# A fused encoder step: probabilities by key block with the sinks as a score column, and the sums' reciprocals as a power on GpSimd

## The chip, the cores and the metric

One core of one Trainium2 chip runs the whole step. The metric is the device time of one execution in microseconds (us). Engines are called as in the profile: PE is TensorE, DVE is VectorE, ACT is ScalarE, POOL is GpSimd, SP is SyncE (it only issues DMAs). "L434" is line 434 of the kernel; the changed kernel has its own line numbers.

## The reference

One layer, 320 rows (256 of a new stream and 64 of a running one), width 2048, in fp32. A combined projection `z = rmsnorm(x) @ W_in` gives queries, keys, values and the gMLP's two halves. The attention has 16 heads of 64 channels, two key/value heads, chunks of 64 rows that see their own and the two chunks before, a relative-position bias and a learned sink per head:

```python
def sink_attention(q, k, v, bias, sinks, valid=None):
    s = jnp.einsum('...qhgd,...khd->...hgqk', q, k).astype(jnp.float32) * (HEAD_DIM ** -0.5) + bias
    if valid is not None:
        s = jnp.where(valid, s, NEG_INF)
    sink = sinks.astype(jnp.float32)[..., None]
    m = jnp.maximum(jnp.max(s, axis=-1), sink)
    p = jnp.exp(s - m[..., None])
    w = p / (jnp.sum(p, axis=-1, keepdims=True) + jnp.exp(sink - m)[..., None])
    return jnp.einsum('...hgqk,...khd->...qhgd', w.astype(v.dtype), v)
```

Queries and keys are RMS-normalised per head. The gMLP half normalises `v`, mixes it over 128 positions and gates `u` with it. Both results are normalised, joined and projected by `W_out` with a residual, then comes a squared-ReLU MLP of width 8192 with its residual.

## The kernel before

Everything is kept transposed: channels on the 128 partitions, the 320 rows along the free dimension. To reach fp32 precision, every weight piece of 4 x 128 x 256 is split into a high part (`w_hi`, by ACT, L115) and a rest (`w_lo`, by DVE, L116), the activations likewise, and each weight block takes three matmuls of 128x128 by 320 columns (L141; L237 for the first). `product` makes 256 output columns from 16 such blocks in four pieces; there are 8160 of these wide matmuls, and they run in one stream from the start to the end.

All smaller PE work is put between pieces of that stream by hand: `between_pieces` names functions that run behind the given piece, and `issue_after` fixes the order. What stands on DVE, ACT and POOL is ordered by a scheduler at build time from a model of the durations; on the chip each engine works through its list strictly in that order.

Attention works on ten units: five query chunks (64 keys, 128, and three times 192) for each of two key/value heads. `attend(i)` is called twice per 256 projected columns and does three things on PE: it transposes the probabilities of unit i-2 into two `misc` banks (L472), forms the scores of unit i in two banks (L420), and multiplies the transposed probabilities of unit i-3 with the values (L485). There are only two `misc` banks and two score banks, so each attend needs those of the one before to be emptied. Behind the PE part of unit i comes `softmax`, on the other engines: DVE scales the scores by the queries' norms and adds the bias into a tile `s` (L434, two buffers), takes the maximum over the keys (L438), joins it with the sinks, negates it and forms the sinks' distance (L440 to L444); ACT takes the exponentials with their sums `den` (L449) and that of the sink (L445); DVE adds the two and takes the reciprocal (L451, L452); POOL multiplies all of `s` by it in one instruction (L453). At the end ACT and DVE add up the values' two halves into `ao` (L495, L497), and DVE copies the transposed probabilities out of the `misc` banks (L501).

Between the attends lie the v columns of the gMLP: `gelu2` (DVE L518, L521 and L524, ACT, POOL L522), the sums of squares `acc_v` (POOL L513) and the gains (POOL L541). Behind the last attend, `rows_norm` makes the row norms of v (DVE L169, a power on POOL L171), and `by_rows` transposes v in two groups (L553), which ACT evicts with those norms as scale (L555).

Another power runs on POOL for the queries' norms (L334), 20 values per partition.

Of the kernel before, what the change touches and what calls it, by code (L numbers as in the profile page):

```python
# [15 lines left out]
P = 128  # L16
# [14 lines left out]
def hymba_step_kernel(ctx: ExitStack, tc: tile.TileContext, i, o):  # L31
# [53 lines left out]
    nc.gpsimd.dma_start(out=tab, in_=i["table"].rearrange("b h -> h b"))  # L85
    inv_1k = const.tile([P, 1], F32, name="inv_1k")
# [16 lines left out]
    loads, between, rests, steps, narrow, carry = [], [], [], [], [], []  # L103
# [18 lines left out]
    def products(w, k0, nk, c0, ps, rh, rl, deep=None, between_pieces={}, halves_behind={}):  # L122
# [6 lines left out]
        for a in range(0, nk, 4):  # L129
# [3 lines left out]
            with tc.issue_after(halves_behind[a // 4]()) if a // 4 in halves_behind else nullcontext():  # L133
                high, low = halves(raw, hi, lo)
# [39 lines left out]
    def two_parts(acc):  # L174
        hl = sm.tile([P, 2, T], F32R, name="n_hl", tag="w2", bufs=4)
        hi, lo = hl[:, 0], hl[:, 1]
        nc.scalar.activation(out=hi, in_=acc, func=AF.Copy)
        rests.append(nc.vector.tensor_tensor(out=lo, in0=acc, in1=hi.bitcast(F32), op=ALU.subtract).ins)
        return hi, lo

# [112 lines left out]

    kv = sm.tile([P, 2, T], F32, name="kv", tag="w2", bufs=4)
    with tc.issue_after(steps[-1][0]):
# [5 lines left out]
    def evict_q(g, q_ps):  # L301
# [11 lines left out]
        nc.scalar.activation(out=sq, in_=qg, func=AF.Square)  # L313
        return sq

    q_dram = dram.tile([2, 2, 2, 2, T], F32, name="q_dram")
    r_at = lambda g, b, p: (g // 2) * 20 + p * 10 + (g % 2) * 5 + b

    def norm_q(h, sqs):

        st = misc()
        for c in range(4):
            mm = nc.tensor.matmul(out=st[c * 32:(c + 1) * 32, 0:T], lhsT=hone, rhs=sqs[c // 2][:, :, c % 2], start=True, stop=True)  # L323
        narrow.append(mm.ins)
        rows = sm.tile([P, T], F32, name="q_rows", tag="w1", bufs=3)
        nc.scalar.activation(out=rows, in_=st[:, 0:T], func=AF.Copy)
# [11 lines left out]
    v0, v64, v128, vC, vD, w2, w3, w4 = (vz[:, x] for x in range(8))  # L338

# [24 lines left out]
    nc.scalar.activation(out=ksq, in_=zk, func=AF.Square)  # L364
    q0_sq = evict_q(0, q0_ps)
# [3 lines left out]
    def first_norms():  # L369
        rstd(ksq, mean_hd, EPS, rk)  # L370
        q1_sq.append(evict_q(1, q1_ps))

    def keys():
        for dst, c in ((kn[:, 0:256], slice(0, 256)), (kn[:, 384:448], slice(256, 320))):
            nc.vector.scalar_tensor_tensor(out=dst, in0=zk[:, c], scalar=g_k, in1=rk[:, c], op0=ALU.mult, op1=ALU.mult)
        for h in range(2):
# [8 lines left out]
        values(0, 1)  # L385

    q2_ps = product(w_in, 0, KT, 512, xh, xl,
                    between_pieces={0: first_norms, 1: lambda: norm_q(0, (q0_sq, q1_sq[0])), 2: keys, 3: lambda: values(2, 3, 4, 5)},
                    halves_behind={1: lambda: q0_out})
# [5 lines left out]
        (0, 0, 64, 128, None, (v0, w2)),  # L395
# [354 lines left out]
```

## Time and profile before

| | |
|---|---|
| median of 3 runs | 1239.93 us (1239.65 to 1240.73) |
| the profiled execution | 1239.04 us, span 1237.3 us |
| PE busy | 1232.8 us, 100% of the span |
| DVE, ACT, POOL busy | 663.6, 492.0, 114.0 us |
| chain that ended last | 99% PE, 93% of it `acc` L141 |
| clock of PE granted | full speed over the whole span |

The span is that of the traced instructions; the time also holds 1.7 us around it. In the groups, "idle before" is the time in which an engine had nothing to do ahead of these instructions, and what it waited for. In timelines the columns are start, duration, engine, line, operation, output and inputs with shapes; the bracket tells a wait and what ended it. Durations include the time in which an instruction stands still after it has started.

### The profile page before, as it was taken

How to read it: one execution, taken by the hardware profiler on the slowest of the kernel's cores; microseconds unless marked ns; L12 is line 12 of the kernel's file. 1: busy time of each engine (PE TensorE's matmuls, PEld its weight loads, DVE VectorE, ACT ScalarE, POOL GpSimd, SP SyncE). 2: the span in 40 equal slices, each digit the busy share in tenths (PEclk: the TensorE clock that was granted, in tenths of full speed). 3: DMA queues.
4: the chain of work that ended last, by engine and by line, in shares of the span. 5: the costliest groups of instructions: out<-in, count | busy, mean ns of one | idle time of the engine just before them, and what ended most of it. 6: DMA issues, size and time to landing. Idle time of an engine off the chain costs nothing.

```text
span 1237.3 us, 20626 instructions
## 1 busy us (share of the span) xinstructions
PE 1232.8 (100%) x8666; PEld 1225.0 (99%) x8666; DVE 663.6 (54%) x796; ACT 492.0 (40%) x652; POOL 114.0 (9%) x139
## 2 busy tenths in 40 slices
PE   9999999999999999999999999999999999999998
PEld 9999999999999999999999999999999999999998
DVE  7877778877864444444444444444444434444343
ACT  7446566435534432333434332344432333433321
POOL 3127454102200000000000000000000000000000
PEclk9999999999999999999999999999999999999999
DMA  9753346444555444454444444455444454445540
GB/s 282 226 148 104 104 138 195 153 154 141 151 152 153 153 147 145 152 154 149 146 149 153 154 150 143 151 154 152 147 147 151 154 151 144 150 152 164 172 161 33
DMA packets 187934, 188.03 MB, mean 152 GB/s; under 512 B 7616, under 2 KB 187376, under 8 KB 187840
## 3 DMA queue, kind: packets, MB, share of 16 engines
q1 hardware_dynamic: 186544, 185.48, 48.7%
q0 software_dynamic: 864, 0.98, 0.4%
q8 instruction: 68, 1.11, 0.4%
q10 hardware_dynamic: 432, 0.24, 0.1%
q14 instruction: 26, 0.21, 0.1%
HBM read 183.10 MB, written 3.35 MB: 151 GB/s over the span
## 4 chain that ended last, share of the span: by engine, by line
PE 99%; DVE 0%; issue 0%; ACT 0%; DVEq 0%
PE acc L141 93%; PE q_ps L237 1%; PE misc L141 1%; PE acc L237 1%; PE s_ps L420 1%; PE misc L472 0%; PE misc L83 0%; PE misc L485 0%; PE s_ps L485 0%; PE g_ps L566 0%; PE misc L566 0%; PE misc L553 0%; PE misc L323 0%; ACT s L449 0%; ACT w_hi L115 0%
## 5 line engine op out<-in xcount | busy, mean ns | idle before, releaser
L116 DVE TENSOR_TENSOR w_lo<-w_raw,w_hi 128x1024 fp32r<-128x1024 f32 x332 | 416.0, 1253 | 422.7 <-ACT w_hi L115 414.1
L115 ACT ACTIVATE w_hi<-w_raw 128x1024 fp32r<-128x1024 f32 x332 | 351.8, 1060 | 670.9 <-PE acc L141 646.7
L141 PE MATMUL acc<-H2H,w_lo 128*128 128x320 f32 x1024 | 316.4, 309 | 0.0
L141 PE MATMUL acc<-H2H,w_hi 128*128 128x320 f32 x1024 | 316.4, 309 | 0.0
L141 PE MATMUL acc<-H2L,w_hi 128*128 128x320 f32 x1024 | 316.4, 309 | 0.0
L141 PE MATMUL acc<-FH,w_hi 128*128 128x320 f32 x992 | 306.5, 309 | 0.0
L141 PE MATMUL acc<-FL,w_hi 128*128 128x320 f32 x992 | 306.5, 309 | 0.0
L141 PE MATMUL acc<-FH,w_lo 128*128 128x320 f32 x992 | 306.5, 309 | 0.0
L141 PEld LDWEIGHTS acc<-H2H,w_hi 128*128 128x128 f32 x1024 | 192.2, 188 | 0.0
L141 PEld LDWEIGHTS acc<-H2L,w_hi 128*128 128x128 f32 x1024 | 192.2, 188 | 0.0
L141 PEld LDWEIGHTS acc<-H2H,w_lo 128*128 128x128 f32 x1024 | 192.2, 188 | 0.0
L141 PEld LDWEIGHTS acc<-FH,w_hi 128*128 128x128 f32 x992 | 186.2, 188 | 0.0
L141 PEld LDWEIGHTS acc<-FL,w_hi 128*128 128x128 f32 x992 | 186.2, 188 | 0.0
L141 PEld LDWEIGHTS acc<-FH,w_lo 128*128 128x128 f32 x992 | 186.2, 188 | 0.0
L141 PE MATMUL acc<-XH,w_hi 128*128 128x320 f32 x352 | 110.7, 314 | 0.0
L141 PE MATMUL acc<-XH,w_lo 128*128 128x320 f32 x352 | 108.8, 309 | 0.0
L141 PE MATMUL acc<-XL,w_hi 128*128 128x320 f32 x352 | 108.7, 309 | 0.0
L141 PEld LDWEIGHTS acc<-XH,w_hi 128*128 128x128 f32 x352 | 66.1, 188 | 3.1 <-issue 3.0
L141 PEld LDWEIGHTS acc<-XL,w_hi 128*128 128x128 f32 x352 | 66.1, 188 | 0.0
L141 PEld LDWEIGHTS acc<-XH,w_lo 128*128 128x128 f32 x352 | 66.1, 188 | 0.0
L658 DVE SCALAR_TENSOR_TENSOR tf<-acc,r 128x640 f32<-128x640 f32 x32 | 26.4, 824 | 41.8 <-PE acc L141 41.8
L673 DVE TENSOR_TENSOR xT<-xT,acc 128x640 f32<-128x640 f32 x31 | 25.5, 821 | 41.8 <-PE acc L141 41.8
(227 smaller groups left out, 1086.3 us busy)
## 6 DMA issues: line engine op xcount, KB each, us to landing
w_raw<-in_w_up SPq DMA_DIRECT2D x128, 512.0 KB
w_raw<-in_w_down SPq DMA_DIRECT2D x128, 512.0 KB
w_raw<-in_w_in SPq DMA_DIRECT2D x44, 512.0 KB
w_raw<-in_w_out SPq DMA_DIRECT2D x32, 512.0 KB
w_first<-in_w_in SPq DMA_DIRECT2D x14, 256.0 KB
out_yT<-xT SPq DMA_DIRECT2D x7, 320.0 KB
xT<-in_xT SPq DMA_DIRECT2D x8, 160.0 KB
xT<-in_xT SPq DMA_DIRECT2D x4, 320.0 KB
```

Source lines behind the costliest of these rows:

```text
L115: return (pin(nc.scalar.activation(out=hi, in_=raw, func=AF.Copy)).ins, pin(nc.vector.tensor_tensor(out=lo, in0=raw, in1=hi.bitcast(F32), ...
L116: pin(nc.vector.tensor_tensor(out=lo, in0=raw, in1=hi.bitcast(F32), op=ALU.subtract)).ins)
L141: mm = nc.tensor.matmul(out=out, lhsT=w_[:, k, g * P:(g + 1) * P], rhs=r_(kk), start=(kk == 0 and x == 0), stop=(kk == nk - 1 and x == 2))
L237: mm = nc.tensor.matmul(out=ps[:, 0:T], lhsT=w_[:, j, k, g * P:(g + 1) * P], rhs=r_(a + k), start=(a + k == 0 and x == 0), stop=(a + k == ...
L420: mm = nc.tensor.matmul(out=s_ps[p][x * HD:(x + 1) * HD, j * nk:(j + 1) * nk], lhsT=qT[hs, blk_, a + x], rhs=kz[hs, kv, k0:k0 + nk], start ...
L658: nc.vector.scalar_tensor_tensor(out=t, in0=ps[:, :, 0:T], scalar=0.0, in1=r2[:, None, :].to_broadcast([P, 2, T]), op0=ALU.max, op1=ALU.mult)
L673: nc.vector.tensor_tensor(out=xT[:, a, c], in0=xT[:, a, c], in1=p, op=ALU.add)
```

## The change

The scores' tile `s` gets one more key column that holds the sinks, copied by DVE (L444 of the changed kernel). The maximum is taken over keys and sink at once, already negated, and the exponentials with their sums run over the sink's column too. So the steps for the sink alone, the addition and DVE's reciprocal go. The reciprocal is a power of -1 on POOL (L457), from a constant tile `minus`. POOL then writes the probabilities into a new tile `pr` in two instructions (L461), ordered by blocks of 64 keys. `s` has one buffer in place of two, `pr` has two.

The transposes take one block of 64 keys for each half of the partitions (L483: 64 rows by 128 columns of weights, 64 columns of output), so that each value half is multiplied and summed in its own bank, and `ao` needs one copy per half in place of copy and addition. The value tiles are made from three transposes in place of six, moved out by four ACT copies. The parts of two sums of squares are formed earlier, and the second `norm_q` runs in the same place as `attend(2)`.

The diff, cut to what is spoken of:

```diff
@@ -83,6 +83,8 @@
         nc.tensor.matmul(out=warm_ps[:, 0:256], lhsT=nc.const_aps.tensor(0.0, [P, P], F32),
                          rhs=nc.const_aps.tensor(0.0, [P, 256], F32), start=True, stop=True)
     nc.gpsimd.dma_start(out=tab, in_=i["table"].rearrange("b h -> h b"))
+    minus = const.tile([P, 2, 2], F32, name="minus")
+    nc.vector.memset(minus, -1.0)
...
-    kzv = blk("kzv", [P, 2304])
+    kzv = blk("kzv", [P, 2560])
...
-    vz = kzv[:, 896:1920].rearrange("p (x h d) -> p x h d", x=8, h=2)
-    cv = i["cv"].rearrange("k (h d) -> k h d", h=2)
-    between.extend(((vz[:, 3], cv), (vz[0:HD, 4], cv[HD:P]), (vz[HD:P, 7], cv[0:HD])))
+    vz = kzv[:, 896:1792].rearrange("p (x h d) -> p x h d", x=7, h=2)
+    cv = i["cv"].rearrange("(x k) (h d) -> k x h d", x=2, h=2)
+    between.extend(((vz[0:HD, 5:7], cv), (vz[HD:P, 5:7], cv)))
...
-        with tc.issue_after(steps[min(8 + k // 2, 11)][0]):
+        with tc.issue_after(steps[min(5 + k // 2, 11)][0]):
             nc.scalar.activation(out=sq, in_=xT[:, k:k + 2], func=AF.Square)
...
-    def values(*xs):
-        for x, vps in zip(xs, [score_bank(1, "vps"), misc()] if len(xs) == 2 else banks(4)):
-            t0 = (0, 64, 128, -64, 192, 256)[x]
-            n = min(P, T - t0)
-            with tc.issue_after(narrow[-1]):
-                mm = nc.tensor.transpose(out=vps[0:n, 0:P], in_=kvx[:, 448 + t0:448 + t0 + n], identity=ident)
-            narrow.append(mm.ins)
-            for dst, r in (((v0, slice(0, P)), (w3, slice(HD, P))), ((v64, slice(0, P)),),
-                           ((v128, slice(0, P)), (w2, slice(0, HD))), ((w2, slice(HD, P)),),
-                           ((w3, slice(0, HD)), (vD, slice(HD, P))), ((w4, slice(0, HD)),))[x]:
-                nc.vector.tensor_copy(out=dst[r], in_=vps[r, 0:P].rearrange("k (h d) -> k h d", h=2))
-
-
-    q1_ps = product(w_in, 0, KT, 256, xh, xl, between_pieces={0: lambda: rstd(ssq, mean_dm, EPS, rx)},
-                    halves_behind={2: lambda: rests[-1]})
+    def values():
+        with tc.issue_after(narrow[-1]):
+            vps = score_bank(1, "vps").rearrange("k (x d) -> k x d", x=4)
+            for x, (t0, n) in enumerate(TT):
+                mm = nc.tensor.transpose(out=vps[0:n, x], in_=vT[:, t0:t0 + n], identity=ident)
+        narrow.append(mm.ins)
+        turned[:] = [vps]
+
+    def values_out():
+        vps = turned[0]
+        low, high = slice(0, HD), slice(HD, P)
+        for dst, to, of in ((low, 0, low), (high, 1, high), (high, 0, low), (low, 1, high)):
+            with tc.issue_after(turned[1]):
+                nc.scalar.activation(out=vz[dst, to:5:2].rearrange("k x h d -> k x (h d)"), in_=vps[of, 0:3 - to], func=AF.Copy)
+
...
     q2_ps = product(w_in, 0, KT, 512, xh, xl,
-                    between_pieces={0: first_norms, 1: lambda: norm_q(0, (q0_sq, q1_sq[0])), 2: keys, 3: lambda: values(2, 3, 4, 5)},
-                    halves_behind={1: lambda: q0_out})
+                    between_pieces={0: first_norms, 1: lambda: (values(), norm_q(0, (q0_sq, q1_sq[0])), values_out()), 2: keys},
+                    halves_behind={1: lambda: (q0_out, *parts_k[2:4])})
...
@@ -425,80 +439,72 @@
         blk_, kv = units[u]
         q0, k0, nk, b0 = blocks[blk_][0:4]
         js = slice(2 * kv, 2 * kv + 2)
-        s = at.tile([P, 2, 2, 192], F32, name="s", tag="s", bufs=2)
-
-        sv = s[:, :, :, 0:nk] if nk > HD else \
-            s.rearrange("x p j k -> x p (j k)")[:, :, P:2 * P].rearrange("x p (j k) -> x p j k", j=2)
+        s = at.tile([P, 2, 2, 193], F32, name="s", tag="s", bufs=1)
+        sv, se = s[:, :, :, 0:nk], s[:, :, :, 0:nk + 1]
+        nc.vector.tensor_copy(out=s[:, :, :, nk], in_=sinks_pj[:, :, js])
         for p in range(2):
             for j in range(2):
                 nc.vector.scalar_tensor_tensor(out=sv[:, p, j], in0=s_ps[p][:, j * nk:(j + 1) * nk],
                                                scalar=rq[:, r_at(2 * kv + j, blk_, p):r_at(2 * kv + j, blk_, p) + 1],
                                                in1=bias[:, p, 2 * kv + j, b0:b0 + nk], op0=ALU.mult, op1=ALU.add)
-        m = at.tile([P, 2, 2], F32, name="m", tag="m")
-        nc.vector.tensor_reduce(out=m, in_=sv, axis=AX.X, op=ALU.max)
-        sk = sinks_pj[:, :, js]
-        nc.vector.tensor_tensor(out=m, in0=m, in1=sk, op=ALU.max)
         nm = at.tile([P, 2, 2], F32, name="nm", tag="nm")
-        nc.vector.tensor_scalar(out=nm, in0=m, scalar1=-1.0, scalar2=None, op0=ALU.mult)
-        es = at.tile([P, 2, 2], F32, name="es", tag="es")
-        nc.vector.tensor_tensor(out=es, in0=sk, in1=m, op=ALU.subtract)
-        nc.scalar.activation(out=es, in_=es, func=AF.Exp)
+        nc.vector.tensor_reduce(out=nm, in_=se, axis=AX.X, op=ALU.max, negate=True)
         den = at.tile([P, 2, 2], F32, name="den", tag="den")
         for p in range(2):
             for j in range(2):
-                nc.scalar.activation(out=sv[:, p, j], in_=sv[:, p, j], func=AF.Exp, bias=nm[:, p, j:j + 1],
+                nc.scalar.activation(out=se[:, p, j], in_=se[:, p, j], func=AF.Exp, bias=nm[:, p, j:j + 1],
                                      accum_out=den[:, p, j:j + 1])
-        nc.vector.tensor_tensor(out=den, in0=den, in1=es, op=ALU.add)
-        nc.vector.reciprocal(out=den, in_=den)
-        ready[:] = [nc.gpsimd.tensor_tensor(out=sv, in0=sv, in1=den[:, :, :, None].to_broadcast([P, 2, 2, nk]),
-                                            op=ALU.mult).ins]
-        probs[u] = s
+        nc.gpsimd.tensor_tensor(out=den, in0=den, in1=minus, op=ALU.pow)
+        pr = at.tile([P, 2, 3, 2, HD], F32, name="pr", tag="pr", bufs=2)
+        ns = nk // HD
+        for p in range(2):
+            ready[:] = [nc.gpsimd.tensor_tensor(out=pr[:, p, 0:ns].rearrange("x n j k -> x j n k"),
+                                                in0=sv[:, p].rearrange("x j (n k) -> x j n k", k=HD),
+                                                in1=den[:, p, :, None, None].to_broadcast([P, 2, ns, HD]), op=ALU.mult).ins]
+        probs[u] = pr
 
     def attend(i):
 
         t, v = i - 2, i - 3
         t, v = t if 0 <= t < 10 else None, v if 0 <= v < 10 else None
-        bank = [misc(), misc()] if t is not None else None
-        s_ps = [score_bank(p) for p in range(2)]
+        bank = [misc(), misc()] if t is not None else [score_bank(r) for r in range(2)]
+        s_ps = [score_bank(p) for p in range(2)] if i < 10 else None
+        hs = [slice(r * HD, (r + 1) * HD) for r in range(2)]
 
         def behind(mms):
             with tc.issue_after(narrow[-1]):
                 narrow.append([mm() for mm in mms][-1].ins)
 
         if t is not None:
-            s = probs.pop(t).rearrange("x p j k -> x p (j k)")
-            nk = blocks[units[t][0]][2]
-            cols = ((P, 2),) if nk == HD else ((0, 0), (192, 1)) if nk == P else ((0, 0), (256, 1), (P, 2))
-            behind([lambda p=p, x=x, c=c: nc.tensor.transpose(out=bank[p][:, x * P:(x + 1) * P], in_=s[:, p, c:c + P],
-                                                              identity=ident) for p in range(2) for c, x in cols])
+            s = probs.pop(t)
+            subs = range(len(blocks[units[t][0]][4]))
+
+            def turn(p, n, x):
+                return nc.tensor.transpose(out=bank[x][:, (p * 3 + n) * HD:(p * 3 + n + 1) * HD],
+                                           in_=s[hs[x], p, n].rearrange("x j k -> x (j k)"), identity=ident[hs[x], hs[x]])
+
+            behind([lambda p=p, n=n, x=x: turn(p, n, x) for p in range(2) for n in subs for x in range(2)])
         if i < 10:
             behind([lambda: scores(i, s_ps)])
         if v is not None:
             blk_, kv = units[v]
-            q0, va, vb = (blocks[blk_][x] for x in (0, 4, 5))
-            hs = [slice(r * HD, (r + 1) * HD) for r in range(2)]
-            side = {(r, j): bank[r][:, 384:512] if bank and j == 0 else s_ps[r][:, 384:512] if j else s_ps[r][:, 0:P]
-                    for r in range(2) for j in range(2)}
-
-            def part(r, j, p, span):
-                lhsT, c = (va[j][hs[r], kv], slice(j * P, (j + 1) * P)) if span < 2 else (vb[j][hs[j], kv], slice(256, 384))
-                return nc.tensor.matmul(out=side[r, j][hs[p]], lhsT=lhsT, rhs=pts[v % 2][p][hs[r], c],
-                                        start=span < 2 or va is None, stop=span == 2 or vb is None or r != j)
-
-            turns = [x for x in (0, 2, 1) if (va, va, vb)[x] is not None]
-            behind([lambda r=r, p=p, x=x: part(r, 1 - r if x == 1 else r, p, x) for x in turns for r in range(2) for p in range(2)])
+            q0, tiles = blocks[blk_][0], blocks[blk_][4]
+            side = [b[:, 384:512] for b in bank]
+            behind([lambda n=n, x=x, j=j, p=p: nc.tensor.matmul(out=side[j][hs[p]], lhsT=vz[hs[j], x, kv],
+                                                                rhs=pts[v % 2][hs[j], :, p, n], start=n == 0,
+                                                                stop=n == len(tiles) - 1)
+                    for n, x in enumerate(tiles) for j in range(2) for p in range(2)])
         if i < 10:
             softmax(i, s_ps)
         if v is not None:
             for j in range(2):
                 dst = ao[:, 4 * kv + 2 * j:4 * kv + 2 * j + 2, q0:q0 + 64]
-                nc.scalar.activation(out=dst, in_=side[j, j].rearrange("p (a q) -> p a q", a=2), func=AF.Copy)
-                if va is not None:
-                    nc.vector.tensor_tensor(out=dst, in0=dst, in1=side[1 - j, j].rearrange("p (a q) -> p a q", a=2), op=ALU.add)
+                nc.scalar.activation(out=dst, in_=side[j].rearrange("p (a q) -> p a q", a=2), func=AF.Copy)
         if t is not None:
-            for p in range(2):
-                c = slice(min(x for _, x in cols) * P, (max(x for _, x in cols) + 1) * P)
-                nc.vector.tensor_copy(out=pts[t % 2][p][:, c], in_=bank[p][:, c])
+            for x in range(2):
+                ns = slice(0, len(subs))
+                nc.vector.tensor_copy(out=pts[t % 2][:, x, :, ns],
+                                      in_=bank[x][:, 0:384].rearrange("k (p n q) -> k p n q", p=2, n=3)[:, :, ns])
 
     q3_ps = product(w_in, 0, KT, 768, xh, xl,
                     between_pieces={1: lambda: attend(0), 3: lambda: attend(1)})
@@ -528,11 +534,10 @@
         return at.tile([P, TP], F32, name=name, tag="ssq_rows", bufs=1)
 
     acc_v = sums_rows("acc_v")
-    gvs = at.tile([P, 8, HD], F32, name="gvs", bufs=1)
+    gvs = room[:, 2048:2560].rearrange("p (a t) -> p a t", a=8)
     for g in range(4):
         v_ps = product(w_in, 0, KT, 2304 + g * 256, xh, xl, between_pieces={
-            1: lambda: attend(2 * g + 2), 2: lambda: norm_q(1, (q2_sq, q3_sq)) if g == 0 else None,
-            3: lambda: attend(2 * g + 3)})
+            1: lambda: (attend(2 * g + 2), norm_q(1, (q2_sq, q3_sq)) if g == 0 else None), 3: lambda: attend(2 * g + 3)})
         gelu2(v_ps, gv[:, 2 * g:2 * g + 2])
         for a in range(2 * g, 2 * g + 2):
             add_square(acc_v, gv[:, a], a == 0)
```

On POOL, around the product of unit 5 (64 keys; `gv` and `acc_v` are gains and sums of the v columns, `den` the sums of the exponentials), there stood:

```order
L522 TENSOR_TENSOR gc<-gc,z 128x640
L541 TENSOR_SCALAR gvs<-gv,cols 128x64 x2
L513 TENSOR_TENSOR acc_v<-acc_v,sq 128x320
L541 TENSOR_SCALAR gv<-gv,cols 128x256 x2
L513 TENSOR_TENSOR acc_v<-acc_v,sq 128x320
L453 TENSOR_TENSOR s<-s,den 128x2x128
L453 TENSOR_TENSOR s<-s,den 128x4x128
```

and now:

```order
L528 TENSOR_TENSOR gc<-gc,z 128x640
L546 TENSOR_SCALAR vnat<-gv,cols 128x64 x2
L457 TENSOR_TENSOR den<-den,minus 128x4
L519 TENSOR_TENSOR acc_v<-acc_v,sq 128x320
L546 TENSOR_SCALAR gv<-gv,cols 128x256 x2
L461 TENSOR_TENSOR pr<-s,den 128x128 x2
L519 TENSOR_TENSOR acc_v<-acc_v,sq 128x320
L457 TENSOR_TENSOR den<-den,minus 128x4
L461 TENSOR_TENSOR pr<-s,den 128x2x2x64 x2
```

The gains and one sum, which ran ahead of the product and needed nothing of the unit, now stand between the unit's power and its two products.

On DVE, at the next unit (128 keys, `attend(6)`), there stood:

```order
L116 TENSOR_TENSOR w_lo<-w_raw,w_hi 128x1024
L434 SCALAR_TENSOR_TENSOR s<-s_ps_1606,rq,bias 128x128 x2
L501 COPY kzv<-misc 128x384
L434 SCALAR_TENSOR_TENSOR s<-s_ps_1605,rq,bias 128x128 x2
L497 TENSOR_TENSOR ao<-ao,misc 128x2x64
L501 COPY vnat<-misc 128x384
```

and now:

```order
L118 TENSOR_TENSOR w_lo<-w_raw,w_hi 128x1024 x2
L444 COPY s<-sinks 128x4
L447 SCALAR_TENSOR_TENSOR s<-s_ps_1586,rq,bias 128x128 x2
L447 SCALAR_TENSOR_TENSOR s<-s_ps_1587,rq,bias 128x128 x2
L506 COPY kzv<-misc 128x384
L451 TENSOR_REDUCE nm<-s 128x4
L506 COPY kzv<-misc 128x384
```

The copy of the sinks into the single `s` stands ahead of the score evictions and of both bank copies. In the units of 192 keys a part of the weights has its place inside that stretch (unit 8):

```order
L444 COPY s<-sinks 128x4
L118 TENSOR_TENSOR w_lo<-w_raw,w_hi 128x1024
L447 SCALAR_TENSOR_TENSOR s<-s_ps_1831,rq,bias 128x192 x2
L447 SCALAR_TENSOR_TENSOR s<-s_ps_1832,rq,bias 128x192 x2
L506 COPY kzv<-misc 128x2x128 x2
```

where before `w_lo` stood ahead of the evictions and nothing tied these to POOL's product of the unit before. On POOL, behind the last unit's softmax, two `acc_v` sums and a copy (L513, L542) that stood ahead of its product now follow it (L519, L547), ahead of the `gc` of the first u columns.

More of the change, by code (lines that the diff above doesn't have):

```diff
@@ L100, in hymba_step_kernel @@
     nc.vector.memset(hone[HD:P, 1:2], 1.0)
-    loads, between, rests, steps, narrow, carry = [], [], [], [], [], []
+    firsts, loads, between, rests, steps, narrow, carry = [], [], [], [], [], [], []
     def load(out, in_):
@@ L132, in products @@
             load(raw, wv[:, k0 + a:k0 + a + 4, c0:c0 + 256])
-            with tc.issue_after(halves_behind[a // 4]()) if a // 4 in halves_behind else nullcontext():
+            with ExitStack() as order:
+                for ins in halves_behind[a // 4]() if a // 4 in halves_behind else ():
+                    order.enter_context(tc.issue_after(ins))
                 high, low = halves(raw, hi, lo)
@@ L176, in two_parts, with parts_of @@
         hi, lo = hl[:, 0], hl[:, 1]
-        nc.scalar.activation(out=hi, in_=acc, func=AF.Copy)
+        firsts.append(nc.scalar.activation(out=hi, in_=acc, func=AF.Copy).ins)
         rests.append(nc.vector.tensor_tensor(out=lo, in0=acc, in1=hi.bitcast(F32), op=ALU.subtract).ins)
         return hi, lo
+    def parts_of(acc):
+        hi, lo = two_parts(acc)
+        return hi, lo, firsts[-1], rests[-1]
     def rstd(acc, mean, eps, out):
@@ L321, in norm_q @@
         st = misc()
-        for c in range(4):
-            mm = nc.tensor.matmul(out=st[c * 32:(c + 1) * 32, 0:T], lhsT=hone, rhs=sqs[c // 2][:, :, c % 2], start=True, stop=True)
+        with tc.issue_after(narrow[-1]):
+            for c in range(4):
+                mm = nc.tensor.matmul(out=st[c * 32:(c + 1) * 32, 0:T], lhsT=hone, rhs=sqs[c // 2][:, :, c % 2], start=True,
+                                      stop=True)
         narrow.append(mm.ins)
         rows = sm.tile([P, T], F32, name="q_rows", tag="w1", bufs=3)
-        nc.scalar.activation(out=rows, in_=st[:, 0:T], func=AF.Copy)
+        turned.append(nc.scalar.activation(out=rows, in_=st[:, 0:T], func=AF.Copy).ins)
         for c in range(4):
@@ L405, in hymba_step_kernel @@
     probs, ready = {}, []
-    room = blk("vnat", [P, 2432])
+    room = blk("vnat", [P, 2560])
     vnat = room[:, 0:2048].rearrange("p (t c) -> p t c", t=2)
-    pt1 = at.tile([P, 768], F32, name="pt1", bufs=1)
-    pts = [(kzv[:, 1920:2304], room[:, 2048:2432]), (pt1[:, 0:384], pt1[:, 384:768])]
+    pts = [kzv[:, 1792:2560].rearrange("k (x p n q) -> k x p n q", x=2, p=2, n=3),
+           at.tile([P, 2, 2, 3, HD], F32, name="pt1", bufs=1)]
     def scores(u, s_ps):
```

25 lines of the change are left out of this document (15 added, 10 removed).

## The prediction

> **What bounds the kernel now.** I read the page first: its busy times and its chain.
>
> ```profile
> span 1237.3 us, 20626 instructions
> PE 1232.8 (100%) x8666; PEld 1225.0 (99%) x8666; DVE 663.6 (54%) x796; ACT 492.0 (40%) x652; POOL 114.0 (9%) x139
> PE 99%; DVE 0%; issue 0%; ACT 0%; DVEq 0%
> ```
>
> TensorE (PE) is the whole chain. Then the windows: one far behind the attention, and one over the stretch in which eight of the ten attention units run.
>
> ```profile
> 400.00:800.00 400.00, 400.00 (x2730) 400.00 (x2729) 173.61 (x156) 139.15 (x140) 0.00 (x0) 1.00 0.48 150
> 90.00:180.00 90.00, 89.66 (x846) 85.17 (x845) 72.71 (x149) 51.90 (x138) 54.61 (x48) 1.00 0.41 116
> ```
>
> A weight matmul costs 400/2730 = 146.5 ns; the change leaves all of these in place. So it can act in two ways only: the few PE instructions that attention puts into this stream change price, or another engine becomes so late that PE stands still. In 90 to 180 us DVE is busy 81% and POOL 61%, so the second way is near. The timeline of PE at one `attend` (first wide row to last) shows the first way:
>
> ```profile
> 130.99 0.31 PE L141 MATMUL acc<-XH,w_lo 128*128 128x320 f32 x1
> 131.14 0.38 PE L472 MATMUL misc<-ident,s 128*128 128x128 f32 x2
> 131.45 0.88 PE L420 MATMUL s_ps<-kzv,qT 64*64 64x192 f32 x16
> 132.92 0.41 PE L141 MATMUL acc<-XH,w_hi 128*128 128x320 f32 x1
> 133.17 0.31 PE L141 MATMUL acc<-XL,w_hi 128*128 128x320 f32 x1
> 122.00 0.82 PE L472 MATMUL misc<-ident,s 128*128 128x128 f32 x6
> 148.77 0.82 PE L472 MATMUL misc<-ident,s 128*128 128x128 f32 x6
> L472 PE MATMUL misc<-ident,s 128*128 128x128 f32 x48 | 7.1, 273 | 0.3 <-DVE vnat L501 0.3
> ```
>
> Two things to see. Six transposes take 0.82 us, one 0.273: a spacing of (0.82 - 0.273)/5 = 0.11 us. And the only wait of PE here, 0.3 us, is for a DVE copy (L501) that empties a `misc` bank. Three attends lie between 122.00 and 148.77: PE needs one every 8.92 us, and that is the time the other engines have for a softmax.
>
> **The change, part by part.** *PE's own work.* 48 transposes become 48 pairs, on the two row halves. No row shows such a pair. The nearest: score matmuls on four quarters, 16 records in 0.88 us, run together. If a pair does too, streaming 64 columns instead of 128, it takes about 0.065 us and 48 x 0.045 = 2.1 us go; at most half, 2.6; nothing if weight loading keeps 0.11 per pair. The new tile shape adds a change of shape at each of ten attends. Leaving the quarters costs 133.17 - 132.92 - 0.147 = 0.10 us behind the first wide matmul and some 0.05 to 0.1 ahead of it, so 0.15 x 10 = +1.5 (0 to +1.8). The values' six transposes become three (-0.33), and the second `norm_q` shares the attend's group (-0.15). Sum -1.1, between -3.1 and +1.3 (+6.6 if halves do not overlap at all: 48 x 0.11 more).
>
> *Instructions taken off DVE and ACT.* Per unit five four-element DVE operations, two additions to `ao` and an exponential go; a four-element copy comes. Nothing of these is on PE's chain, so by themselves they are worth 0.
>
> *POOL and the single buffer.* Before, `s` had two buffers. Now it has one: the copy of the sinks of unit u+1 must wait for POOL's writing of `pr` of unit u. Behind that copy on DVE stand the unit's score evictions, the bank copies (now L506) and later `w_lo` parts; the next attend's transposes wait for those banks. On POOL a power now stands ahead of `pr`, and in places gains and sums between the two. Their prices:
>
> ```profile
> L453 POOL TENSOR_TENSOR s<-s,den 128x768 f32<-128x768 f32 x6 | 8.8, 1468 | 5.3 <-PE misc L485 3.3 <-DVE den L452 1.9
> L453 POOL TENSOR_TENSOR s<-s,den 128x256 f32<-128x256 f32 x2 | 2.2, 1105 | 4.9 <-DVE den L452 4.9
> L334 POOL TENSOR_TENSOR rq<-r_q,nhalf 128x20 f32<-128x20 f32 x2 | 7.6, 3820 | 2.0 <-DVE r_q L333 1.9
> 105.56 4.07 POOL L334 TENSOR_TENSOR rq<-r_q,nhalf 128x20 f32<-128x20 f32 x1
> 178.47 1.79 POOL L171 TENSOR_TENSOR rs_rows<-r_rows,nhalf 128x3 f32<-128x3 f32 x1 [0.50 <-DVE r_rows L169]
> 178.31 1.21 DVE L116 TENSOR_TENSOR w_lo<-w_raw,w_hi 128x1024 fp32r<-128x1024 f32 x1
> 179.45 0.28 DVE L497 TENSOR_TENSOR ao<-ao,s_ps 128x128 f32<-128x128 f32 x1
> ```
>
> No row has a power of four elements. The shorter one of 20 took 2 x 3.82 - 4.07 = 3.57 us. The one of three took 1.79, but a `w_lo` ran beside it until 179.45; if it stood behind that, its own part is 178.47 + 1.79 - 179.45 = 0.81. Through 0.81 at three and 3.57 at 20 four give 0.97 us, which I take (bounds 0.8 and 1.9). The products: 1.47 us for 768; of the two for 256 one took 1.60 (next fence), so the other 0.61. That is 0.19 + 0.00166 per element, and half-size pieces cost 0.40 and 0.83. The added POOL work per unit is 0.97 + 0.19 = 1.16 us.
>
> *The first late unit.* Unit 5 (64 keys), timelines of DVE, ACT and POOL:
>
> ```profile
> 123.36 0.19 ACT L449 ACTIVATION_READ_ACCUMULATOR s<-s,nm 128x1 f32 x1
> 121.22 0.88 POOL L513 TENSOR_TENSOR acc_v<-acc_v,sq 128x320 f32<-128x320 f32 x1
> 122.08 2.37 POOL L541 TENSOR_SCALAR gv<-gv,cols 128x256 f32<-128x256 f32 x2
> 125.26 1.60 POOL L453 TENSOR_TENSOR s<-s,den 128x256 f32<-128x256 f32 x1
> 124.53 1.85 DVE L116 TENSOR_TENSOR w_lo<-w_raw,w_hi 128x1024 fp32r<-128x1024 f32 x1 [0.57 <-ACT w_hi L115]
> 126.30 0.60 DVE L434 SCALAR_TENSOR_TENSOR s<-s_ps,rq,bias 128x128 f32<-128x128 f32 x2
> 127.29 0.59 DVE L434 SCALAR_TENSOR_TENSOR s<-s_ps,rq,bias 128x128 f32<-128x128 f32 x2
> 128.00 0.55 DVE L501 COPY vnat<-misc 128x384 f32<-128x384 f32 x1
> ```
>
> The denominators stand at 123.55. Before, POOL had already begun `acc_v` and both `gv` there; now these stand between the power and `pr`. So `pr` ends at 123.55 + 0.97 + 0.88 + 2.37 + 2 x 0.40 = 128.6 if nothing blocks. A `w_lo` and a POOL product hold each other up (1.85 us here against 1.21 above; 1.60 against 0.61): two `w_lo` fall in, 1.14 us each, so the upper end is 130.9. Then the sink copy (0.16), the evictions (0.60 + 0.59) and two bank copies (1.0): banks free between 131.0 and 133.3, against transposes at 131.14. That is 0 to 2.2 us of wait at `attend(7)`; before, the banks were free at 128.55. I take 2.0, near the upper end, since both stand directly ahead of that sink copy on DVE's queue.
>
> *The units of 192 keys.* The loop from one sink copy to the next:
>
> ```profile
> L434 DVE SCALAR_TENSOR_TENSOR s<-s_ps,rq,bias x40: 264/401/410, 71.9 to 157.0; 128x192 f32<-128x192 f32 x24, 128x64 f32<-128x64 f32 x8, 128x128 f32<-128x128 f32 x8
> L438 DVE TENSOR_REDUCE m<-s x10: 401/934/954, 73.8 to 158.2; 128x4 f32<-128x768 f32 x6, 128x4 f32<-128x256 f32 x2, 128x4 f32<-128x512 f32 x2
> L449 ACT ACTIVATE s<-s,nm 128x192 f32<-128x192 f32 x24 | 10.6, 442 | 2.0 <-DVE nm L442 1.3 <-DVE es L444 0.8
> 129.83 0.40 ACT L449 ACTIVATE s<-s,nm 128x128 f32<-128x128 f32 x1 [2.56 <-DVE es L444]
> 131.61 0.16 DVE L451 TENSOR_TENSOR den<-den,es 128x4 f32<-128x4 f32 x1 [1.81 <-ACT s L449]
> ```
>
> Copy 0.16; four evictions 1.3 (0.40 each, less the overlap that the pairs above show); bank copies 1.0; reduce 0.93; exponentials 1.9 (1.78 for 128 keys from 129.83 to 131.61, adjusted for width and the one that goes); power 0.97; `pr` 1.66; hand-overs between engines 0.3 (an estimate). Sum 8.2 us against PE's 8.92: it fits only if nothing else gets in. In the units of 192 keys on DVE's queue a `w_lo` (1.14) stands between sink copy and evictions: 9.35, +0.4 per unit, for `attend(8)` to `attend(10)` +1.2 (0 if it hides; +4.7 if a second one blocks POOL, 10.5 each).
>
> *By rows.* The last place is the second group of `by_rows` (L553):
>
> ```profile
> 160.52 2.53 POOL L513 TENSOR_TENSOR acc_v<-acc_v,sq 128x320 f32<-128x320 f32 x2 [3.20 <-ACT sq L512]
> 163.11 0.23 POOL L542 COPY acc_v<-acc_v 128x64 f32<-128x64 f32 x1
> 172.69 1.58 POOL L522 TENSOR_TENSOR gc<-gc,z 128x640 f32<-128x640 f32 x1 [0.83 <-DVE gc L521]
> 180.30 0.69 ACT L555 ACTIVATE vnat<-misc,rs_rows 128x512 f32<-128x512 f32 x1 [0.27 <-POOL rs_rows L171]
> 181.35 1.04 PE L553 MATMUL misc<-ident,gv 128*128 128x128 f32 x8
> ```
>
> ACT's eviction ends at 180.99, PE uses its bank at 181.35: 0.36 us of slack. The two sums and the copy ran ahead of unit 9's product; now they stand behind it, so `gc` comes later by 2.53 + 0.23 + 1.16 - 0.83 (the idle time) = 3.1 us. Through ACT, DVE's `gu` (in whose queue `r_rows` stands) and the power this reaches the bank: 3.1 - 0.36 = 2.7 us of wait (0 to 4).
>
> **The sum.** Where PE waits, its own savings ahead of the wait vanish into it. So the terms are 2.0 + 1.2 + 2.7 = +5.9, and PE's -1.1 counts only where nothing waits. Against the profiled execution (1239.04: its span and 1.7 us around it) that is 1244.9; the median of the runs lies 0.9 higher, so **1246**.
>
> **The rivals.** (1) *No new wait.* The place is the loop: it decides below 8.9 us, which a power of 0.5 us or less, or a `w_lo` that lets POOL go on, would give. For it: 8.2 without obstacles, and banks free 2.6 us early at `attend(7)` before. Against it: 1.85 and 1.60 above. Time: 1239.93 - 1.1 = 1238.8; -3.1 at best, 1236.8. Chance 0.27: 0.17 within 0.2% (2.5 us, which a measurement hardly tells from no change), 0.10 faster. (2) *POOL and DVE block each other in full*, twice a unit: loop 10.5, 4.7 us in place of 1.2, and the same excess of 1.6 for two units of 192 keys ahead of `attend(7)`: 1246 + 3.5 + 3.2 = 1252.7. For it: 72.7 + 54.6 + 8 x 1.16 us of both engines in 90. Against: before, the two met in only some units (1.60 for one product of 256, 0.61 for the other). Chance 0.13. (3) *The halves do not overlap*: a transpose still loads 128 columns of weights, and 96 at 0.11 us take 5.3 us more. With the waits absorbing about half of that: 1248.5. The Trainium skill, "TensorE: Matmul & The Clock Gate", section on LDWEIGHTS, says the load's time goes with columns and not with contraction rows; by it a half-height transpose saves nothing alone. The trace's 0.11 us spacing at 128 columns agrees; whether two halves load together no row shows. Chance 0.10. The forecast keeps 0.50.
>
> Faster 0.10, same 0.17, slower 0.73. The likeliest case alone spans 1242 to 1249 (its three terms at their bounds, mostly). The range takes in most of rivals 1 and 2: **1238 to 1252**.
>
> **What would show it.** Right: PE idle ahead of the transposes (now L483), released by the copies L506, 1 us or more near 132 and some tenths near 141, 150 and 161; DVE idle at the copy of the sinks, released by POOL's `pr`; the power near 1 us, `pr` 0.40 to 0.83; and idle time at L558 near 187, released by ACT's eviction. Wrong: no idle time of PE between 120 and 190 us (rival 1), a power under 0.5 us, or waits whose releaser is not a bank copy. Transposes that start one by one, 0.11 us apart, would show rival 3; waits of over 1 us at every attend from the fourth on, rival 2.

## The result, and the profile after

The changed kernel takes **1246.4 us** (median of 5 runs, 1245.6 to 1247.16) against 1239.93: a ratio of 1.0053, 95% interval 1.0043 to 1.0064. It is slower by 6.5 us. The profiled execution is the slowest of the five (1247.16, span 1245.4), so against the span of before (1237.3) there are 8.1 us to find.

The page of the changed kernel, the lines that answer to those of before:

```profile
span 1245.4 us, 20647 instructions
PE 1235.3 (99%) x8711; PEld 1225.7 (98%) x8711; DVE 651.1 (52%) x732; ACT 491.2 (39%) x646; POOL 133.5 (11%) x159
PE 93%; POOL 3%; issue 2%; DVE 1%; DMA 0%; ACT 0%; POOLq 0%; DVEq 0%; ACTq 0%
```

DVE has 12.5 us less to do, POOL 19.5 us more, and the chain now leaves PE for POOL. The groups show where PE stands still, and the waits over 85 to 200 us why:

```profile
L483 PE MATMUL misc<-ident,pr 64*128 64x64 f32 x96 | 6.3, 234 | 4.2 <-DVE pt L506 2.8 <-DVE kzv L506 1.0
L558 PE MATMUL misc<-ident,gv 128*128 128x128 f32 x12 | 1.9, 281 | 1.3 <-ACT vnat L560 1.3
DVE s L444 <- POOL pr L461: 9.4, 8, 2.4
L457 POOL TENSOR_TENSOR den<-den,minus 128x4 f32<-128x4 f32 x10 | 10.2, 1025 | 26.0 <-ACT s L455 26.0
L461 POOL TENSOR_TENSOR pr<-s,den 128x384 f32<-128x384 f32 x12 | 15.9, 1342 | 0.3
L444 DVE COPY s<-sinks 128x4 f32<-128x4 f32 x10 | 5.1, 509 | 10.0 <-POOL pr L461 10.0
```

The transposes wait for bank copies (L506), these stand on DVE behind the copy of the sinks (L444), and that waits for POOL's `pr`. The power takes 1.03 us. A half-width product takes 1.34 us on the mean; the shortest take 0.82.

How long PE needs from the start of the last wide matmul ahead of each group to the first one behind it, in us, read from the PE timelines of three kernels (the third is an experiment below, with two buffers of `s` and the reciprocal on DVE):

| group | before | changed | two buffers, DVE reciprocal |
|---|---|---|---|
| `attend(5)` | 1.95 | 2.47 | 1.81 |
| `attend(6)` | 2.15 | 4.08 | 2.01 |
| `attend(7)` | 1.93 | 3.29 | 2.01 |
| `attend(8)` | 1.71 | 2.27 | 1.66 |
| `attend(9)` | 2.14 | 2.41 | 2.00 |
| `attend(10)` | 1.73 | 3.07 | 1.63 |
| `attend(11)` | 2.24 | 1.57 | 1.57 |
| second group of `by_rows` | 1.81 | 3.28 | 2.39 |

The changed kernel loses 6.8 us here against before. Another 1.3 us are lost in no wait at all: behind `attend(6)` the wide matmuls run at half their rate. The timeline of PE there, and the windows ahead of it, in it and behind it:

```profile
122.31 0.31 PE L145 MATMUL acc<-XH,w_lo 128*128 128x320 f32 x1
124.05 0.96 PE L483 MATMUL misc<-ident,pr 64*128 64x64 f32 x12 [1.43 <-DVE pt L506]
126.39 0.63 PE L145 MATMUL acc<-XH,w_hi 128*128 128x320 f32 x1
126.82 0.47 PE L145 MATMUL acc<-XL,w_hi 128*128 128x320 f32 x1
122.00:126.40 4.40, 2.84 (x58) 2.07 (x56) 3.43 (x9) 2.34 (x10) 1.52 (x4) 0.95 0.14 49
126.40:129.40 3.00, 3.00 (x15) 3.00 (x12) 1.46 (x2) 2.77 (x6) 3.00 (x3) 0.51 0.01 3
129.40:134.00 4.60, 4.60 (x34) 4.60 (x33) 2.22 (x4) 0.00 (x0) 4.24 (x5) 1.00 0.74 218
```

The granted clock is the number behind the POOL column: 0.51 for 3 us, then 1.00. Within that stretch the wide matmuls start 267 ns apart instead of 146.5. All five runs show a mean clock of 0.998 or 0.999, where the kernel before shows 1.0 in all but 2 of the 49 runs measured beside the experiments, so it is not an accident of this one.

What made `attend(6)` late stands on DVE and POOL just ahead of it:

```profile
118.39 2.73 POOL L461 TENSOR_TENSOR pr<-s,den 128x384 f32<-128x384 f32 x2
121.08 1.57 POOL L528 TENSOR_TENSOR gc<-gc,z 128x640 f32<-128x640 f32 x1
118.18 1.22 DVE L118 TENSOR_TENSOR w_lo<-w_raw,w_hi 128x1024 fp32r<-128x1024 f32 x1 [1.10 <-ACT w_hi L117]
121.15 1.53 DVE L444 COPY s<-sinks 128x4 f32<-128x4 f32 x1 [0.72 <-POOL pr L461]
122.59 0.85 DVE L447 SCALAR_TENSOR_TENSOR s<-s_ps,rq,bias 128x64 f32<-128x64 f32 x4
123.36 1.00 DVE L506 COPY pt<-misc 128x384 f32<-128x384 f32 x2
112.76 0.17 DVE L444 COPY s<-sinks 128x4 f32<-128x4 f32 x1 [2.32 <-POOL pr L461]
```

The product of unit 4 takes 2.73 us for two halves because a `w_lo` has come first. Then the copy of four sinks per partition, 0.17 us a unit earlier, takes 1.53: it ends with POOL's `gc`. The bank copies end at 124.4, and PE begins its transposes at 124.05, when the first of the two banks is free.

### The profile page after: what moved, and what is told of

Its sections match the earlier page's. It is cut to its first block, busy times and chain, and to the rows that moved or that the text cites. A ratio compares the mean times of both kernels' runs of the same rounds, so it can differ in the third digit from the quotient of the medians.

```text
span 1245.4 us, 20647 instructions
## 1 busy us (share of the span) xinstructions
PE 1235.3 (99%) x8711; PEld 1225.7 (98%) x8711; DVE 651.1 (52%) x732; ACT 491.2 (39%) x646; POOL 133.5 (11%) x159
## 4 chain that ended last, share of the span: by engine, by line
PE 93%; POOL 3%; issue 2%; DVE 1%; DMA 0%; ACT 0%; POOLq 0%; DVEq 0%; ACTq 0%
PE acc L145 88%; PE q_ps L245 1%; PE acc L245 1%; PE misc L145 1%; POOL pr L461 1%; POOL gv L546 1%; POOL den L457 0%; DMA r_q<-q_dram 0%; POOL acc_v L519 0%; POOL vnat L546 0%; PE misc L83 0%; DVE s L447 0%; DVE w_lo L118 0%; POOL q_dram L341 0%; ACT w_hi L117 0%
```

## The experiments

The theory: the single `s` and the power make POOL part of a loop that PE waits for; the rivals were POOL and DVE in each other's way whatever the buffers, and dearer PE instructions. All ratios below are against the kernel before, measured beside each run; the interval stands in brackets.

**One part undone at a time.** Two buffers for `s`, laid into free columns of another tile:

```diff
-    kvx = blk("kvx", [P, 768])
+    kvx = blk("kvx", [P, 2560])
-        s = at.tile([P, 2, 2, 193], F32, name="s", tag="s", bufs=1)
+        s = kvx[:, 768 + 772 * (u % 2):1540 + 772 * (u % 2)].rearrange("x (p j k) -> x p j k", p=2, j=2)
```

> The changed kernel with two buffers for s again (they lie in unused columns of the keys' and values' tile), the power and all else kept. Theory A (the single s ties the next unit's evictions and bank copies to POOL's writing of pr): PE's waits at the attends go, some 6 of 8 us, and the wait at by_rows stays in part (0 to 1.5 us): 1239 to 1241.5, and the copy of the sinks no longer waits for pr. Theory B (POOL has too much to do, and blocks DVE, whatever the buffers): pr is as late as now and the transposes wait for pr itself: 1244 to 1247. Theory C (PE's own instructions became dearer): 1246, with no idle time of PE left to explain it.

Measured: 1239.3 us, ratio 0.9994 (0.9985 to 1.0002). Its groups:

```profile
L483 PE MATMUL misc<-ident,pr 64*128 64x64 f32 x96 | 5.4, 233 | 0.0
L558 PE MATMUL misc<-ident,gv 128*128 128x128 f32 x12 | 1.9, 282 | 1.2 <-ACT vnat L560 1.2
L457 POOL TENSOR_TENSOR den<-den,minus 128x4 f32<-128x4 f32 x10 | 10.2, 1020 | 19.8 <-ACT kvx L455 19.8
DVE kvx L444 <- POOL pr L461: 3.7, 6, 1.1
```

Every wait at the attends is gone with the power still there, and that at `by_rows` stays. That is the time and the waits of theory A, and not those of B and C. One sign of A did not come: the copy of the sinks still waits for `pr`, 3.7 us in six units (last line, 85 to 200 us). It is now the copy for the next unit and can stand elsewhere on DVE's list: at units 3 and 4 it stands behind the unit's evictions (those of unit 4 start at 108.14, while `pr` of unit 3 ends at 111.43), at the others still ahead of them, where `pr` comes in time. So two buffers also gave DVE another order, and no run holds that order fixed.

The reciprocal back on DVE, with `s` single:

```diff
-        nc.gpsimd.tensor_tensor(out=den, in0=den, in1=minus, op=ALU.pow)
+        nc.vector.reciprocal(out=den, in_=den)
```

> The changed kernel with the reciprocal on DVE again (0.18 us there) in place of the power on POOL, s single as in the change. Theory A with the power as the decisive part of the loop: about 0.9 us less per unit, so the loop of 192 keys with one w_lo is 8.5 us against PE's 8.92: waits shrink to 0 to 2 us in all, 1239.5 to 1241.5. If the single buffer with gains and sums between alone is enough for the waits: 1243.5 to 1246.

Measured: 1238.06 us, ratio 0.9984 (0.9975 to 0.9993), which is below the expected interval and faster than both kernels. Its groups:

```profile
L483 PE MATMUL misc<-ident,pr 64*128 64x64 f32 x96 | 5.3, 233 | 0.0
L558 PE MATMUL misc<-ident,gv 128*128 128x128 f32 x12 | 1.9, 282 | 0.4 <-ACT vnat L560 0.4
L461 POOL TENSOR_TENSOR pr<-s,den 128x128 f32<-128x128 f32 x4 | 2.1, 551 | 4.2 <-DVE den L457 3.1 <-PE s_ps L434 1.1
```

Without the power the single buffer costs nothing. Both undone:

> Both: two buffers for s and the reciprocal on DVE; the transposes by half, the value sums and the sinks' column as in the change. Theory A: no wait of PE above 0.3 us at any attend and at most 0.5 at by_rows; what is left is PE's own, forecast -1.1 us: 1238.8, between 1237 and 1240. Theory C: 1241 or more, the transposes and their change of tile shape dearer than before.

Measured: 1238.1 us, ratio 0.9986 (0.9977 to 0.9995). PE waits at no attend, and 0.35 us at `by_rows`, as theory A had it. So the changed kernel's table is complete: power and single `s` 1246.4, power alone 1239.3, single `s` alone 1238.1, neither 1238.1. By these medians the power costs 1.2 us by itself (the intervals of these two runs overlap, but in the traces `by_rows` is 0.85 us longer and `attend(10)` 0.2), the single buffer 0, the two together 8.3.

Undoing either also let the scheduler place the gains of the v columns on POOL behind `pr` of unit 5 instead of between the power and `pr`. To tell that order from the rest, the changed kernel with only this rule extended to all units:

```diff
-                with tc.issue_after(ready[0]) if g == 3 else nullcontext():
+                with tc.issue_after(ready[0]):
```

> The changed kernel, power and single s kept, but the gains of the v columns are ordered behind the products of every unit (the change does so for the last only), so that on POOL only the power, or the power and one sum, stands ahead of pr. If the lateness came from the gains that stand between the power and pr (the first late unit of the forecast): 1238.5 to 1240.5. If the power's own 1.03 us in the loop is what counts: 1243 to 1246, with waits at attend(8) to attend(10) of 0.3 us and more each.

Measured: 1241.57 us, ratio 1.0013 (1.0004 to 1.0022), between the two expectations. The groups:

```profile
L483 PE MATMUL misc<-ident,pr 64*128 64x64 f32 x96 | 5.6, 233 | 2.1 <-DVE pt L506 2.0
L558 PE MATMUL misc<-ident,gv 128*128 128x128 f32 x12 | 1.9, 282 | 1.2 <-ACT vnat L560 1.2
```

The place of the gains is worth 4.8 of the 8.3 us, slow stretch included; the rest is there only with the power. Of that rest 2.3 us go with a second buffer (1241.57 to 1239.3) and 1.2 with the reciprocal on DVE. The waits that stay here are at `attend(6)` and `attend(10)`, 1.3 us each, and at `by_rows`; `attend(8)` and `attend(9)` are clean, where 0.3 us and more were expected.

**The blocked copy.** The copy of the sinks moved from DVE to POOL, behind `pr`:

```diff
-        nc.vector.tensor_copy(out=s[:, :, :, nk], in_=sinks_pj[:, :, js])
+        nc.gpsimd.tensor_copy(out=s[:, :, :, nk], in_=sinks_pj[:, :, js])
```

> The changed kernel with the copy of the sinks' column on POOL, directly behind pr, in place of DVE. On DVE two of these copies stood still for 1.5 us beside POOL's gc, one of them right ahead of the wait at attend(6). If that block is what starts the wait there: attend(6) loses 1.4 us of its wait and the slow matmuls behind it (1.3 us): 1243 to 1244.5, the copy 0.2 us on POOL. If the lateness is set by POOL's list anyway: 1246 to 1247.5, since POOL has one instruction more per unit.

Measured: 1244.46 us, ratio 1.0034 (1.0021 to 1.0046), at the upper end of the first expectation. From the PE timeline, `attend(6)` needs 2.50 us instead of 4.08, with no slow stretch behind it, so the block had its part in that wait. But `attend(7)` now needs 5.30 instead of 3.29, and the slow stretch comes behind that. The copy takes 0.19 us on POOL where nothing holds it up, as I had said, but up to 1.07, and 0.40 on the mean.

**The parts in the kernel before.** Only the power, with the reciprocal's line in `softmax` (L452) replaced by it (`minus` is the constant tile of the change):

```diff
-        nc.vector.reciprocal(out=den, in_=den)
+        nc.gpsimd.tensor_tensor(out=den, in0=den, in1=minus, op=ALU.pow)
```

> The kernel before with the reciprocal as a power on POOL, two buffers of s, nothing else. If the power hurts only together with the single buffer: at the attends nothing; at by_rows, where the slack is 0.36 us, up to 1 us later: 1240 to 1241. If POOL's extra 1 us per unit hurts by itself: 1242 to 1246.

Measured: 1241.15 us, ratio 1.0010 (1.0001 to 1.0018), but not where I had put it. `by_rows` is as before; at `attend(9)` PE waits for POOL's product itself:

```profile
L474 PE MATMUL misc<-ident,s 128*128 128x128 f32 x48 | 7.1, 274 | 1.2 <-POOL s L455 1.2
```

Only the single buffer:

```diff
-        s = at.tile([P, 2, 2, 192], F32, name="s", tag="s", bufs=2)
+        s = at.tile([P, 2, 2, 192], F32, name="s", tag="s", bufs=1)
```

> The kernel before with one buffer for s in place of two, nothing else. If the single buffer hurts only together with the power (what the pair of runs with one part undone each says of the changed kernel): 1239.5 to 1241, no idle time of PE at the transposes above 0.5 us. If the single buffer hurts by itself: 1242 to 1246, with waits for bank copies.

Measured: 1271.18 us, ratio 1.025 (1.0233 to 1.0266). This run does not test what I meant it to. In the kernel before, `s` holds the probabilities until the transposes two attends later, and one buffer ties the next evictions to those. In the changed kernel `pr` holds them, and `s` is free after POOL's product. The timeline at `attend(4)` shows the other loop, in which PE waits twice within one attend:

```profile
110.14 0.87 PE L472 MATMUL misc<-ident,s 128*128 128x128 f32 x6 [2.30 <-POOL s L453]
113.01 1.86 PE L420 MATMUL s_ps<-kzv,qT 64*64 64x192 f32 x11 [2.00 <-DVE s L434]
```

So a single `s` is bearable only because of `pr`; that is all that follows.

**The slow stretch.** Made waits of PE in the MLP of the kernel before, far from attention. The core of the first try, called between two pieces of the `w_up` products (`still` is a tile of zeros; the calls are left out):

```diff
+    def stall(n):
+        st = misc()
+        nc.tensor.transpose(out=st[:, 0:P], in_=still, identity=ident)
+        for _ in range(n):
+            nc.gpsimd.memset(still, 0.0)
+        narrow.append(nc.tensor.transpose(out=st[:, P:2 * P], in_=still, identity=ident).ins)
```

> The kernel before with eight made waits of PE of growing length in the MLP, 14 us apart and far from attention: two 128x128 transposes between which POOL writes the tile they read 2, 4, 5, 6, 7, 8, 10 and 14 times (about 0.25 us each; the output is the same). If an idle time of PE alone lowers its clock, the matmuls behind the longer waits start 267 ns apart for some time, as behind the wait of 1.9 us at attend(6), and those behind the shorter ones stay at 146.5 ns; the waits add 14 us and the slow stretches 1 to 2 us each. If the slow stretch at attend(6) had another cause, all stay at 146.5 ns.

The scheduler moved the second transposes behind other matmuls, so the waits did not grow as planned. What came, at the seventh:

```profile
662.13 0.41 PE L141 MATMUL acc<-H2H,w_hi 128*128 128x320 f32 x1 [0.89 <-ACT w_hi L115]
663.39 0.42 PE L141 MATMUL acc<-H2H,w_lo 128*128 128x320 f32 x1 [0.70 <-DVE w_lo L116]
```

Two waits of 0.89 and 0.70 us within 1.7 us left the clock at 1.00. The second try puts the writes into the way of a weight part (calls left out again):

```diff
+    def stall(n):
+        st = misc()
+        narrow.append(nc.tensor.transpose(out=st[:, 0:P], in_=still, identity=ident).ins)
+        for _ in range(n):
+            nc.gpsimd.memset(still, 0.0)
+
+    def poke(lo):
+        nc.gpsimd.tensor_tensor(out=lo[:, 0, 0:P], in0=lo[:, 0, 0:P].bitcast(F32), in1=still, op=ALU.add)
```

> The kernel before with eight made waits of PE in the MLP, in one piece each this time: PE transposes a tile, POOL then writes that tile 4, 5, 6, 7, 8, 10, 13 and 17 times (0.257 us each) and adds it, all zeros, to a part of w_lo that PE needs 0.6 us behind the transpose. Idle times of about 1.0, 1.2, 1.5, 1.7, 2.0, 2.5, 3.3 and 4.3 us. The waits of the run before, up to 1.2 us, left the matmuls at 146.5 ns. If idle time alone lowers the clock, as behind attend(6) of the changed kernel, the longer of these are followed by matmuls 267 ns apart, from a length between 1.2 and 3.3 us on. If none is, the slow stretch at attend(6) needs more than one wait.

The lengths again came out otherwise: 0.60 us and then 1.01 at the first three places, 0.60 and 0.70 at the other five. But two of the first three are followed by the half rate, for 3.4 us each. The first pair of waits with its windows (with the waits in it, and behind), then two windows that hold the third pair, which is as long, and one behind:

```profile
567.45 0.41 PE L143 MATMUL acc<-H2H,w_hi 128*128 128x320 f32 x1 [0.60 <-ACT w_hi L115]
569.02 0.41 PE L143 MATMUL acc<-H2H,w_lo 128*128 128x320 f32 x1 [1.01 <-POOL w_lo L661]
566.50:569.91 3.41, 1.80 (x11) 1.28 (x10) 1.23 (x1) 0.90 (x1) 2.09 (x5) 1.00 0.46 151
569.91:573.32 3.41, 3.41 (x15) 3.41 (x14) 0.00 (x0) 0.00 (x0) 0.00 (x0) 0.50 0.47 147
600.63:604.05 3.42, 2.50 (x16) 1.97 (x14) 1.13 (x2) 1.06 (x1) 1.28 (x7) 1.00 0.55 164
604.05:607.46 3.41, 2.72 (x18) 2.73 (x19) 0.32 (x1) 0.00 (x0) 0.63 (x1) 1.00 0.51 150
607.46:610.87 3.41, 3.41 (x26) 3.41 (x25) 1.23 (x1) 1.06 (x1) 0.00 (x0) 1.00 0.03 9
```

Idle time of PE by itself can halve its clock for 3.4 us, then. What decides between the first three pairs is where they fall. In these traces the times between two changes of the granted clock are whole multiples of 3.41 us (1, 4, 35 and 165 of them, for instance), so the windows above are cut on that grid. The first and the second pair lie inside one window of the grid each, with 1.61 us idle in it (3.41 less 1.80); the third is split, 0.92 and 0.69. Counted so over the matmul stream, the clock fell behind each of the four windows with 1.56 us idle or more in the changed kernel, in the run with the sink copy on POOL and in the second try, and behind none with less in these and in the first try, where the largest was 1.52. This is no full rule: in the kernel before with one `s` the clock held behind 1.63 and 1.91 us and fell behind 1.00. What else counts there was not found.

## Why the prediction was right, and where its steps were not

The time (1246.4 against 1246), the sign and the mechanism hold: PE waits for bank copies behind a sink copy that waits for `pr`, and for ACT's eviction at `by_rows`. The sum is partly luck, since its terms are off in both directions: it put 5.9 us on top of the profiled execution of before, and the profiled execution of the changed kernel is 8.1 us longer; the medians, to which the forecast was carried over, lie 6.5 apart.

- **The power's price**, read between a 3-element and a 20-element power as 0.97 us: 1.03 measured. The working let the `w_lo` beside the smaller power end at 179.45, but its row gives 178.31 + 1.21 = 179.52; with that the reading would have been 0.91, a little further off. The product pieces of 128 columns, forecast at 0.40 undisturbed, take 0.39 in three of four cases and 1.29 in the fourth.
- **PE's own work**: a pair of half transposes was put at 0.065 us. In the run with neither cause, twelve take 0.59 us:

```profile
147.72 0.31 PE L145 MATMUL acc<-XH,w_lo 128*128 128x320 f32 x1
147.96 0.59 PE L483 MATMUL misc<-ident,pr 64*128 64x64 f32 x12
148.47 0.88 PE L434 MATMUL s_ps<-kzv,qT 64*64 64x192 f32 x16
```

  With the last of them 0.22 long and the first gap 0.11, the other pairs are 0.06 apart: the halves do run together, and rival 3 falls. That run is 1.75 us faster than before (0.6 to 2.9), where -1.1 was forecast. In the changed kernel these savings vanish into the waits, as the forecast said.
- **The first late unit** is the step that was wrong. I named unit 5 and `attend(7)` as the first, +2.0 us, and priced `attend(5)` and `attend(6)` at nothing. Measured: `attend(5)` +0.5, `attend(6)` +1.9, `attend(7)` +1.4. At `attend(5)` PE does not wait for a bank copy either: its score matmuls wait 0.32 us for DVE's eviction (L447) that empties a score bank, behind the same sink copy. The units of 192 keys ahead of it were late already: the sink copy of unit 4 waited for `pr` until 112.76, since at unit 3 too gains and a sum stand between the power and `pr`. Two prices were too low besides. I took the sink copy at 0.16 us, and beside `gc` it took 1.53; and I let `w_lo` block `pr` at unit 5 only, while it does so at unit 4 too (2.73 us for two halves). That was rival 2's excess "for two units of 192 keys ahead of `attend(7)`", 3.2 us there; 2.4 came.
- **The slow stretch**, 1.3 us, was in no term.
- **The units of 192 keys**, `attend(8)` to `attend(10)`: forecast +1.2 us, measured 0.56 + 0.27 + 1.34 = 2.2. They are not 0.4 each but 0.3 to 1.3; that this goes with what else POOL and DVE have in hand at each is likely, but only the place of the gains was varied. `attend(11)`, which no term named, is 0.7 us shorter than before, 0.34 of it a wait that the kernel before had there.
- **`by_rows`**: forecast +2.7 us, measured +1.5, of which 0.6 also stand in the runs without the power. The power for the rows took 1.79 us as before, so the difference lies in how far PE and POOL had both been held up by then; no run took that apart.
- **The rivals**: no new wait at all (1238.8) is nearly what the kernel with either the power or the single buffer undone gives, 1238.1 to 1239.3; only the wait at `by_rows` stays where the power stays. That fits a loop as near its edge as the working had it, 8.2 us of chain against 8.92.
- **The chances**: 0.73 for slower stood on the chain being late at the places of the bank copies, which the trace after shows; the 0.27 for no wait would have been the kernel with the reciprocal left on DVE, or with two buffers.

## What to carry to other kernels

Before a step is moved to an idle engine, write down the loop it joins: here a buffer cut from two to one made POOL's 1 us power and its neighbours in the queue part of what the bound engine waits for, and either cut alone cost at most 1.2 us. In such a loop an engine that is busy 61% of the time, as POOL was before, is not free; what counts is which independent work its queue places between two steps of the chain, and that can be worth more (4.8 us) than the step itself (3.5). If a change bundles several edits, take them apart on the chip: the same value sums, half transposes and sink column without the power are 1.8 us faster than the kernel before.

## What the runs showed of the hardware beyond that

PE's clock can fall to half after idle times that are short: 1.43 us at a bank at `attend(6)` (PE is idle for 1.56 of the 4.4 us of that window), and 0.60 + 1.01 us in a made wait, each followed by 3.4 us at half clock; at `attend(6)` that lost 1.3 us. A wait of PE can so cost nearly twice its length, and whether it does hung, in the made waits, on whether it fell into one window of the clock's 3.41 us grid or across two. The Trainium skill, "TensorE: Matmul & The Clock Gate", in the section on HAM oscillation, warns of idle gaps of more than about 3.4 us; the length of the slow stretches here agrees with that figure, the threshold does not, since 1.56 and 1.61 us of idle time, not all in one piece, were enough.

A DVE copy of four elements per partition within SBUF, the memory of the tiles, took 0.17 us with POOL out of its way, 1.53 us when it started just behind a POOL instruction of 1.57, and 0.83 behind one of 0.87 (at 132.84). The Trainium skill, "SBUF — State Buffer", in the section on who interferes with whom, lists copies among the operations that can take the shared port pair; the trace agrees, and what the copy lost here went with the length of POOL's instruction, not with its own.
